# Weights loaded ahead of their stage, and a retention scan split between DVE and Pool, in an eight-core transformer kernel

## The chip, the cores and the metric

The kernel runs on the 8 cores of one Trainium2 chip, one launch, without communication between cores: cores 0 to 3 work on one latent sequence each, cores 4 to 7 on eight context sequences each. All run the same program on 2048 tokens. The metric is device microseconds of the slowest core. A run has a state: in the slow one, the cores of a die (0 to 3, or 4 to 7) show a lower granted TensorE clock and take some per cent longer. Names of engines: PE multiplies matrices, DVE (vector) and ACT (scalar) work element by element, Pool (GpSimd) can do so too but only issues DMAs in the kernel before, and SP issues the other DMAs. A DMA is a copy between the chip's main memory and SBUF, the memory on the core.

## The reference, cut to what matters

```python
def trunk_layer(x, cond, lp, cache=None, pos=None):      # 4 layers
    h = rms_norm(x, lp['g_pre_mix']) * (1 + sc1) + sh1
    gq, gk, gv, rq, rk, rv, rg, wq, wk, wv = project(h, lp['w_in'])
    glob = ...   # global attention
    win  = ...   # windowed attention
    ret, s_f, s_b = bidir_retention(rq32, rk32, rv32, lg_f, lg_b, ...)
    ret = head_rms(ret) * silu(rg)
    mixed = concat([glob, ret, win]) @ lp['w_out']
    x = x + gt1 * rms_norm(mixed, lp['g_post_mix'])
    ...          # SwiGLU feed-forward, gated residual

def retention_direction(q, k, v, log_gamma, s0):          # 16 chunks of 128 tokens
    def step(s, qkv):
        o = (q k^T * inner_decay) v + (q s) * q_decay     # needs the state before the chunk
        s = s * chunk_decay + (k * k_decay)^T v           # and passes it on
        return s, o
    return lax.scan(step, s0, chunks)
```

The forward direction walks the chunks 0 to 15, the backward one 15 to 0.

## The kernel before

Per layer the stages are: statistics; keys and values (PE needs `hg`, the normalised input, and a weight slot); queries and attention; retention pass A (decayed keys, values, one `U` per chunk); the scan over the chunks; retention pass B; output projection; feed-forward. Barriers, in which each engine waits for all others and for all DMAs, stand after the statistics, the attention, the retention, the output projection and the feed-forward; there is none inside the retention, between pass A, the scan and pass B.

Weights come through `wload`, in pieces, into one of three slots. Every piece writes the same `Buf`, so each waits until the piece before it has landed:

```python
    def wload(pieces, slot=None):
        ...
        for dv, src in pieces:
            S.dma('pool', dv(wslot[i]), src, writes=[WS[i]], semname=f"w{i}")
```

The loads stand in program order at the head of the stage that uses them, after the barrier, in the queue of Pool, which does nothing else. The scan runs on DVE, one direction after the other; partitions 0 to 63 hold the forward state and 64 to 127 the backward one:

```python
for d, rows, order in ((0, slice(0, 64), list(range(16))), (1, slice(64, 128), list(range(15, -1, -1)))):
    for idx, c in enumerate(order):
        S.op('act', ... activation(out=STb[rows, c, :], in_=srun[rows, :], func=AF.Copy) ...)   # state for pass B
        S.op('dve', ... tensor_tensor(out=U[rows, c, :], in0=U[rows, c, :], in1=srun[rows, :], op=ALU.add) ...)
        S.op('dve', ... tensor_tensor(out=U[rows, c, :], in0=U[rows, c, :], in1=gam[rows, :], op=ALU.mult) ...)
        if idx < 15:
            S.op('dve', ... tensor_scalar(out=srun[rows, :], in0=U[rows, c, :], scalar1=tabs[...], op0=ALU.mult) ...)
# pass B, first uses: emit_h(...) on DVE and ACT, rq projection on PE, then
S.mm(ps[ob]..., qs..., STb[:, c, ...], False, True, reads=[QS, STB[c]], ...)      # c = 0 first
...
S.barrier()
for c in range(6):                       # output projection: 14 pieces of w_out, then PE may start
    S.dma('pool', wo[0:64, c, :], w_out_d[...], writes=[WO], semname='wo')
    S.dma('pool', wo[64:128, c, :], w_out_d[...], writes=[WO], semname='wo')
...
```

The softmax here doesn't subtract the row's maximum and nothing guards it: scores larger than these inputs give would overflow.

Of the kernel before, what the change touches and what calls it, by code (L numbers as in the profile page):

```python
# [8 lines left out]
ALU = mybir.AluOpType  # L9
# [109 lines left out]
def build(stop=None):  # L119
# [202 lines left out]
    def normrope(l, g, gcol, ropeT, ROPE, final_fn):  # L322
        for p in normrope_ph(l, g, gcol, ropeT, ROPE, final_fn):
            p()

    def ck(name):
        if stop == name:
            raise _Stop()

    try:  # L330
        ck('prologue')
        emit_mod(0)
        ck('mod0')
        for l in range(L):
# [4 lines left out]
            with nc.sbuf_tensor(f"kTg{l}", [128, 2, 2304], BF16) as kTg, nc.sbuf_tensor(f"kTw{l}", [128, 2, 2304], BF16) as kTw, \  # L339
# [11 lines left out]
                for kvh in range(2):  # L351
# [4 lines left out]
                ck('s1a')  # L356
                wt, WT = wload([
                    (lambda s_: wview(s_, 512)[:, :, 0:64], wsrc(w_in_d, l, GK, 64)),
                    (lambda s_: wview(s_, 512)[:, :, 64:128], wsrc(w_in_d, l, WK, 64)),
                    (lambda s_: wview(s_, 512)[:, :, 128:192], wsrc(w_in_d, l, GK + 64, 64)),  # L360
                    (lambda s_: wview(s_, 512)[:, :, 192:256], wsrc(w_in_d, l, WK + 64, 64)),
                    (lambda s_: wview(s_, 512)[:, :, 256:384], wsrc(w_in_d, l, GV, 128)),
                    (lambda s_: wview(s_, 512)[:, :, 384:512], wsrc(w_in_d, l, WV, 128)),
                ], slot=0)
                for g in range(NG):
# [15 lines left out]
                    for kvh in range(2):  # L381
# [3 lines left out]
                        def fin(kn, KN, kvh=kvh, gs=gs):  # L385
# [6 lines left out]
                ck(f's1_{l}')  # L392
                w0, W0 = wload([(lambda s_, h=h: wview(s_, 512)[:, :, h * 128:h * 128 + 64], wsrc(w_in_d, l, GQ + h * 64, 64)) for h in range(4)] +
                               [(lambda s_, h=h: wview(s_, 512)[:, :, h * 128 + 64:h * 128 + 128], wsrc(w_in_d, l, WQ + h * 64, 64)) for h in range(4)], slot=1)
                w1, W1 = wload([(lambda s_, h=h: wview(s_, 512)[:, :, (h - 4) * 128:(h - 4) * 128 + 64], wsrc(w_in_d, l, GQ + h * 64, 64)) for h in (4, 5)] +
                               [(lambda s_, h=h: wview(s_, 512)[:, :, (h - 4) * 128 + 64:(h - 4) * 128 + 128], wsrc(w_in_d, l, WQ + h * 64, 64)) for h in (4, 5)], slot=2)

                def qproj_prep(g):
# [20 lines left out]
                def attn(g, nxt):  # L419
# [3 lines left out]
                    def npt():  # L423
                        i = pc[0] % 4; pc[0] += 1
                        return i
                    deferred = []

# [121 lines left out]
            with nc.sbuf_tensor(f"rkT{l}", [128, 2, NT], BF16) as rkT, nc.sbuf_tensor(f"rv{l}", [128, 16, 256], BF16) as rv, \  # L549
# [11 lines left out]
                kdec = rtab[:, 1024:1536]  # L561
                gam = rtab[:, 1536:1792]
                lg = rsm[:, 0:8]; lgmix = rsm[:, 8:12]; kd8 = rsm[:, 16:24]; g8 = rsm[:, 24:28]
                S.op('act', lambda e: e.activation(out=lg, in_=sm(l, 82, 8), func=AF.Exp, scale=-1.0), reads=[SMALLS], writes=[RSM])
# [16 lines left out]
                for d in range(2):  # L581
# [4 lines left out]
                     reads=[RSM], writes=[RTAB])  # L586
                w0, W0 = wload([(lambda s, h=h, d=d: wview(s, 512)[:, :, h * 128 + d * 64:h * 128 + d * 64 + 64], wsrc(w_in_d, l, RK + h * 64, 64))
                                for h in range(4) for d in range(2)], slot=0)
                w1, W1 = wload([(lambda s: wview(s, 512)[:, :, 0:256], wsrc(w_in_d, l, RV, 256)),
                                (lambda s: wview(s, 512)[:, :, 256:512], wsrc(w_in_d, l, RK, 256))], slot=1)  # L590
                wv0 = wview(w0, 512); wv1 = wview(w1, 512)
                for g in range(NG):
# [32 lines left out]
                    for b in range(4):  # L625
                        if b + 1 < 4:
                            a1_(b + 1)
                        a2_(b)
                ck(f'ra{l}')
                S.dma('sp', srun[0:64, :], st0_d[l, 0], writes=[SRUN[0]], semname='st0a')  # L630
                S.dma('sp', srun[64:128, :], st0_d[l, 1], writes=[SRUN[1]], semname='st0b')
                for d, rows, order in ((0, slice(0, 64), list(range(16))), (1, slice(64, 128), list(range(15, -1, -1)))):
                    for idx, c in enumerate(order):
                        S.op('act', lambda e: e.activation(out=STb[rows, c, :], in_=srun[rows, :], func=AF.Copy), reads=[SRUN[d]], writes=[STB[c]])
                        S.op('dve', lambda e: e.tensor_tensor(out=U[rows, c, :], in0=U[rows, c, :], in1=srun[rows, :], op=ALU.add), reads=[UU[c], SRUN[d]], writes=[UU[c]])
                        S.op('dve', lambda e: e.tensor_tensor(out=U[rows, c, :], in0=U[rows, c, :], in1=gam[rows, :], op=ALU.mult), reads=[UU[c], RTAB], writes=[UU[c]])
                        if idx < 15:
                            cn = order[idx + 1]
                            kc_ = (T_KF if d == 0 else T_KB) + cn
                            S.op('dve', lambda e: e.tensor_scalar(out=srun[rows, :], in0=U[rows, c, :], scalar1=tabs[rows, kc_:kc_ + 1], scalar2=None, op0=ALU.mult),  # L640
                                 reads=[UU[c], TABS], writes=[SRUN[d]])
                for c in range(16):
                    S.dma('sp', ost_d[l, c], U[:, c, :], reads=[UU[c]], semname='ost')
                ck(f'rec{l}')
                w0, W0 = wload([(lambda s, h=h, d=d: wview(s, 512)[:, :, h * 128 + d * 64:h * 128 + d * 64 + 64], wsrc(w_in_d, l, RQ + h * 64, 64))
                                for h in range(4) for d in range(2)], slot=2)
                w1, W1 = wload([(lambda s: wview(s, 512)[:, :, 0:256], wsrc(w_in_d, l, RG, 256))], slot=0)
                wv0 = wview(w0, 512); wv1 = wview(w1, 512)
                for g in range(NG):
# [29 lines left out]
                    def b2_(b, g=g):  # L679
# [4 lines left out]
                        for h in range(4):  # L684
                            S.mm(ps[ob][:, h * 64:(h + 1) * 64], ad[:, h * 128:(h + 1) * 128], rv[:, c, h * 64:(h + 1) * 64], True, False,
                                 reads=[AD, RV_], writes=[PS[ob]])
                            S.mm(ps[ob][:, h * 64:(h + 1) * 64], qs[:, h * 128:(h + 1) * 128], STb[:, c, h * 64:(h + 1) * 64], False, True,
                                 reads=[QS, STB[c]], writes=[PS[ob]])
                        sq_, SQ_ = ntf()
# [28 lines left out]
                    for t_ in range(4 + 2):  # L718
# [4 lines left out]
                        if 0 <= t_ - 2 < 4:  # L723
                            b3_(t_ - 2)
                    S.dma('sp', mscr_d[g, :, 6:8, :], rmt[:], reads=[RMT], semname='ms')
                S.barrier()
            ck(f'r{l}')
            with nc.sbuf_tensor(f"wo{l}", [128, 8, 1024], BF16) as wo, nc.sbuf_tensor(f"mgl{l}", [128, 2, 8, GT], BF16) as mgl, \
                    nc.sbuf_tensor(f"mx{l}", [128, 8, GT], F32) as mx:
                WO = Buf("wo"); MGL = [Buf("mgl0"), Buf("mgl1")]; MX = [Buf(f"mx{j}") for j in range(8)]  # L730
                for c in range(6):
                    S.dma('pool', wo[0:64, c, :], w_out_d[l, c * 64:(c + 1) * 64, :], writes=[WO], semname='wo')
                    S.dma('pool', wo[64:128, c, :], w_out_d[l, 640 + c * 64:640 + (c + 1) * 64, :], writes=[WO], semname='wo')
                S.dma('pool', wo[:, 6, :], w_out_d[l, 384:512, :], writes=[WO], semname='wo')
                S.dma('pool', wo[:, 7, :], w_out_d[l, 512:640, :], writes=[WO], semname='wo')
                for g in range(NG):
# [3 lines left out]
                    for dc in range(8):  # L740
                        pn = "A" if dc % 2 == 0 else "S0"
                        for c in range(8):
                            S.mm(ps[pn][:], wo[:, c, dc * 128:(dc + 1) * 128], mgl[:, mi, c, :], c == 0, c == 7, reads=[WO, MGL[mi]], writes=[PS[pn]])
                        S.op('act', lambda e: e.activation(out=mx[:, dc, :], in_=ps[pn][:], func=AF.Copy), reads=[PS[pn]], writes=[MX[dc]])
# [9 lines left out]
            with nc.sbuf_tensor(f"h2{l}", [128, 8, 1024], BF16) as h2, nc.sbuf_tensor(f"hid{l}", [128, 11, 1024], BF16) as hid, \  # L754
                    nc.sbuf_tensor(f"ff{l}", [128, 8, 1024], F32) as ff:
                H2 = Buf("h2"); HID = [Buf(f"hid{i}") for i in range(11)]; FF = [[Buf(f"ff{j}_{t}") for t in range(2)] for j in range(8)]
                for half in range(2):
# [42 lines left out]
                    for t in range(2):  # L800
# [4 lines left out]
                        for j in range(8):  # L805
                            tt, TT = ntf()
                            S.op('dve', lambda e: e.scalar_tensor_tensor(out=tt[:], in0=ff[:, j, ts], scalar=coef[l][:, 24 + j:25 + j], op0=ALU.mult, in1=rstdA[:, gs], op1=ALU.mult),  # L807
                                 reads=[FF[j][t], COEF[l], RA[g]], writes=[TT])
                            S.op('dve', lambda e: e.tensor_tensor(out=xT[:, j, gs], in0=xT[:, j, gs], in1=tt[:], op=ALU.add), reads=[X[g][j], TT], writes=[X[g][j]])  # L809
                S.barrier()  # L810
    except _Stop:
# [156 lines left out]
```

## Time and profile before

| | before |
|---|---|
| time, 6 runs | 8509.22 us median (8499.23 to 8523.8) |
| busy: PE, ACT, DVE, Pool | 63%, 44%, 26%, 5% |
| granted TensorE clock, all cores | 0.81 to 0.82 |

The shares of busy time are averages over stages with different limits, so they don't say what the change can win. The waits do. These lines are from the waits of the kernel before, slowest core (engine, what it was to write, line, what it waited for: us in all, times, longest):

```profile
PE psR L77 <- ACT hg L274: 394.5, 28, 57.2
PE psA L77 <- DMA wo<-w_out: 230.8, 4, 58.5
PE psR L77 <- DMA wslot<-w_in: 203.8, 4, 52.0
PE psA L77 <- DMA wslot<-w_in: 195.8, 4, 51.0
```

Three waits for weights occur once in each of the 4 layers. The first line is a sum over several places; its longest single wait, 57.2 us, is the scan.

How much of such a wait can be won is read from the timeline: what else would have been ready, and when? At the output projection (start, duration, engine, line, what, and in brackets the idle time before it and its releaser):

```profile
1468.85 0.79 SPq L95 DMA_DIRECT2D mgl<-mscr  x2
1469.37 0.54 POOL L95 DMA_DIRECT2D wo<-w_out  x1 [216.41 <-DMA mscr<-rmt]
1477.11 0.53 POOL L95 DMA_DIRECT2D wo<-w_out  x1 [7.20 <-DMA wo<-w_out]
1480.49 0.52 POOL L95 DMA_DIRECT2D wo<-w_out  x1 [2.85 <-DMA wo<-w_out]
...
1519.61 0.53 POOL L95 DMA_DIRECT2D wo<-w_out  x1 [3.85 <-DMA wo<-w_out]
1523.66 3.57 PE L77 MATMUL psA<-mgl,wo 128*128 128x512 bf16 x8 [58.45 <-DMA wo<-w_out]
```

One issue per 3.2 to 4.4 us after the first gap, each waiting for the landing of the one before. The other input, `mgl` (the concatenated head outputs), was issued first and takes 5.1 us (page, DMA issues). At the key/value projection (first two lines) and at pass A the other input is `hg`, and it was ready long before the weights:

```profile
158.65 6.43 ACT L274 ACTIVATE hg<-tf,mod 128x512 bf16<-128x512 f32 x8 [11.21 <-DVE tf L271]
196.81 3.57 PE L77 MATMUL psA<-hg,wslot 128*128 128x512 bf16 x8 [50.98 <-DMA wslot<-w_in]
...
1130.59 6.43 ACT L274 ACTIVATE hg<-tf,mod 128x512 bf16<-128x512 f32 x8 [1.22 <-DVE tf L271]
1162.47 5.85 PE L77 MATMUL psR<-hg,wslot 128*128 128x512 bf16 x16 [51.74 <-DMA wslot<-w_in]
```

The scan of the same layer, first step, then the end, and pass B's first use of the state:

```profile
1252.03 0.41 DVE L635 TENSOR_TENSOR U<-U,srun 64x256 f32<-64x256 f32 x1
1252.55 0.42 DVE L636 TENSOR_TENSOR U<-U,rtab 64x256 f32<-64x256 f32 x1
1253.44 0.34 DVE L640 TENSOR_SCALAR srun<-U,tabs_sb 64x256 f32<-64x256 f32 x1 [0.47 <-ACT STb L634]
...
1301.95 5.39 DVE L271 SCALAR_TENSOR_TENSOR tf<-xT_sb,coef,rstdA 128x512 f32<-128x512 f32 x8
1309.38 9.43 PE L77 MATMUL psR<-hg,wslot 128*128 128x512 bf16 x32 [56.84 <-ACT hg L274]
1322.78 0.19 PE L77 MATMUL psO<-STb,tb 128*128 128x64 bf16 x1
```

DVE executes in order, so the `h` of pass B (L271) stands behind all 32 steps of the scan: 49.9 us, 1.56 us a step.

### The profile page before, as it was taken

What the parts mean: (1) busy time and instruction counts of PE and PEld (TensorE: products, weight loads), DVE (VectorE), ACT (ScalarE), POOL (GpSimd) and SP (SyncE); (2) the same over time, 40 slices, a digit from 0 to 9 for tenths busy, and PEclk for the clock granted to TensorE, in tenths of its full rate; (3) what the DMA queues carried; (4) which work ended last, traced back from release to release, by engine and by line L of the source; (5) the groups of instructions that cost most, each with busy time, mean ns of one, the idle gap of its engine ahead of it and who ended that gap; (6) DMA issues with size and microseconds to landing.
All of it is one profiled execution on the core that took longest, in us unless ns stands there. A gap on an engine that the chain in (4) does not pass through costs nothing.

```text
span 8509.3 us, 86765 instructions; the slowest of 8 cores (8482.7 to 8509.3 us)
## 1 busy us (share of the span) xinstructions
PE 5320.0 (63%) x26992; PEld 2366.6 (28%) x26992; DVE 2250.3 (26%) x4163; ACT 3729.1 (44%) x6586; POOL 448.8 (5%) x533
## 2 busy tenths in 40 slices
PE   1477743598557773368936776337893676544887
PEld 0133321143223331123412332212341233221333
DVE  0312124212332213322132221432213222152232
ACT  1566633312356663342235666333214666533321
POOL 1000000011100000001100000000110000000000
PEclk8688876799778886679967988668995788876898
DMA  7111120164301112125521111213552000111445
GB/s 125 32 19 19 24 22 28 30 77 61 47 22 21 23 19 32 25 36 71 64 42 20 19 19 26 26 29 40 65 65 44 1 5 8 17 18 33 56 57 91
DMA packets 544142, 314.24 MB, mean 37 GB/s; under 512 B 185296, under 2 KB 519888, under 8 KB 540624
## 3 DMA queue, kind: packets, MB, share of 16 engines
q0 software_dynamic: 502160, 223.64, 22.1%
q1 hardware_dynamic: 41536, 85.05, 2.9%
q8 instruction: 231, 3.78, 0.2%
q14 instruction: 215, 1.76, 0.1%
HBM read 481.92 MB, written 50.33 MB: 63 GB/s over the span
## 4 chain that ended last, share of the span: by engine, by line
PE 52%; ACT 19%; DVE 10%; issue 10%; DMA 8%; ACTq 1%; DVEq 0%; POOL 0%; POOLq 0%; SPq 0%
PE psS L77 17%; PE psA L77 13%; PE psO L77 11%; PE psR L77 7%; ACT pT L461 4%; PE psM L77 3%; DMA wslot<-w_in 3%; ACT hg L274 3%; DMA wo<-w_out 2%; ACT pT L456 2%; DMA wslot<-w_mod 1%; ACT tb L260 1%; DVE tf L807 1%; ACT pT L504 1%; DVE xT_sb L809 1%
## 5 line engine op out<-in xcount | busy, mean ns | idle before, releaser
L77 PE MATMUL psO<-pT,vall 128*128 128x512 bf16 (+1 forms) x2832 | 847.1, 347 | 743.6 <-ACT pT L461 359.7
L461 ACT ACTIVATE pT<-psS,tabs_sb 128x512 bf16<-128x512 f32 x1344 | 901.2, 687 | 383.5 <-PE psS L77 370.3
L77 PE MATMUL psR<-pT,cbf_sb 128*128 128x512 bf16 (+1 forms) x2832 | 856.5, 350 | 0.0
L77 PE MATMUL psA<-h,wslot 128*128 128x512 bf16 x2816 | 677.1, 384 | 205.5 <-ACT h L765 130.3
L77 PE MATMUL psS<-qTg,kTg 128*128 128x512 bf16 x1728 | 690.2, 410 | 12.2 <-ACT qTg L410 12.2
L77 PEld LDWEIGHTS psO<-pT,vall 128*128 128x128 bf16 x2832 | 257.5, 104 | 1520.9 <-issue 1508.9
L77 PE MATMUL psM<-tb,cbf_sb 128*128 128x512 bf16 x768 | 351.4, 478 | 526.1 <-ACT tb L260 301.9
L77 PE MATMUL psS<-h,wslot 128*128 128x512 bf16 x2816 | 665.4, 379 | 0.0
L783 ACT ACTIVATE tf<-psA 128x512 f32<-128x512 f32 x352 | 210.4, 598 | 964.5 <-PE psA L77 939.3
L77 PE MATMUL psR<-hg,wslot 128*128 128x512 bf16 x768 | 238.4, 479 | 598.8 <-ACT hg L274 394.5
L784 DVE TENSOR_TENSOR hid<-tf,psS 128x512 bf16<-128x512 f32 x352 | 241.9, 687 | 1337.6 <-PE psS L77 1251.7
L77 PE MATMUL psA<-hg,wslot 128*128 128x512 bf16 x896 | 284.0, 474 | 366.4 <-DMA wslot<-w_in 195.8
L77 PEld LDWEIGHTS psA<-h,wslot 128*128 128x128 bf16 x2816 | 277.0, 99 | 549.2 <-issue 226.3
L274 ACT ACTIVATE hg<-tf,mod 128x512 bf16<-128x512 f32 x512 | 369.9, 723 | 116.0 <-DVE tf L271 74.3
L456 ACT ACTIVATE pT<-psS,tabs_sb 128x256 bf16<-128x256 f32 x768 | 354.4, 474 | 115.1 <-PE psS L77 71.5
L77 PEld LDWEIGHTS psS<-h,wslot 128*128 128x128 bf16 x2816 | 275.9, 98 | 333.8 <-issue 2.8
L271 DVE SCALAR_TENSOR_TENSOR tf<-xT_sb,coef,rstdA 128x512 f32<-128x512 f32 x512 | 344.3, 743 | 10.5 <-DMA okT<-tf 10.1
L77 PE MATMUL psO<-hid,wslot 128*128 128x512 bf16 x1408 | 324.8, 379 | 0.0
L77 PE MATMUL psS<-hid,wslot 128*128 128x512 bf16 x1408 | 324.8, 379 | 0.0
L507 DVE TENSOR_TENSOR pT<-pT,cbf_sb 128x128 bf16<-128x128 bf16 x360 | 79.0, 220 | 812.2 <-ACT pT L504 811.0
L77 PEld LDWEIGHTS psM<-tb,cbf_sb 128*128 128x128 bf16 x768 | 76.9, 100 | 776.3 <-issue 754.9
L77 PEld LDWEIGHTS psR<-hg,wslot 128*128 128x128 bf16 x768 | 86.9, 118 | 740.4 <-issue 698.8
(146 smaller groups left out, 6983.5 us busy)
## 6 DMA issues: line engine op xcount, KB each, us to landing
wslot<-w_gate_up POOLq DMA_DIRECT2D x160, 512.0 KB, 6.2
wslot<-w_mod POOLq DMA_DIRECT2D x48, 1024.0 KB, 8.3
wslot<-w_down POOLq DMA_DIRECT2D x64, 704.0 KB, 7.1
wslot<-w_in POOLq DMA_DIRECT2D x128, 128.0 KB, 3.5
mgl<-mscr SPq DMA_DIRECT2D x16, 1024.0 KB, 5.1
mscr<-mg SPq DMA_DIRECT2D x16, 768.0 KB, 3.3
xT_sb<-xT SPq DMA_DIRECT2D x32, 256.0 KB, 19.6
ropeT<-rope SPq DMA_DIRECT2D x8, 1024.0 KB, 4.9
```

Source lines behind the costliest of these rows:

```text
L77: inst = self.eng[e].matmul(out, lhsT=lhsT, rhs=rhs, start=start, stop=stop)
L260: S.op('act', lambda e: e.activation(out=q[:], in_=src_fn(j), func=AF.Square), reads=[SRC[j]], writes=[Q])
L271: S.op('dve', lambda e: e.scalar_tensor_tensor(out=t[:], in0=xT[:, j, gs], scalar=coef[l][:, a_off + j:a_off + j + 1], op0=ALU.mult, in1=r ...
L274: S.op('act', lambda e: e.activation(out=hg[hi][:, j, :], in_=t[:], func=AF.Identity, bias=modt[l][:, b_off + j:b_off + j + 1]), reads=[T, ...
L456: S.op('act', lambda e: e.activation(out=pT[:, pi, qh * 256:(qh + 1) * 256], in_=ps[sn][:, qh * 256:(qh + 1) * 256], func=AF.Exp, bias=tco ...
L461: S.op('act', lambda e: e.activation(out=pT[:, pi, :], in_=ps[sn][:], func=AF.Exp, bias=tcol(bc)), reads=[PS[sn], TABS], writes=[PT[pi]])
L504: S.op('act', lambda e: e.activation(out=pT[:, pi, 0:n], in_=ps[sn][:, 0:n], func=AF.Exp), reads=[PS[sn]], writes=[PT[pi]])
L507: S.op('dve', lambda e: e.tensor_tensor(out=pT[:, pi, j * 128:(j + 1) * 128], in0=pT[:, pi, j * 128:(j + 1) * 128], in1=mprev[i % 2], op=A ...
L783: S.op('act', lambda e: e.activation(out=sa[:], in_=ps["A"][:], func=AF.Silu), reads=[PS["A"]], writes=[SA])
L784: S.op('dve', lambda e: e.tensor_tensor(out=hid[:, fi, ts], in0=sa[:], in1=ps["S0"][:], op=ALU.mult), reads=[SA, PS["S0"]], writes=[HID[fi]])
L807: S.op('dve', lambda e: e.scalar_tensor_tensor(out=tt[:], in0=ff[:, j, ts], scalar=coef[l][:, 24 + j:25 + j], op0=ALU.mult, in1=rstdA[:, g ...
L809: S.op('dve', lambda e: e.tensor_tensor(out=xT[:, j, gs], in0=xT[:, j, gs], in1=tt[:], op=ALU.add), reads=[X[g][j], TT], writes=[X[g][j]])
```

## The change

Its intent: load each stage's weights while the stage before still computes, and halve the scan by running its two directions at once, the forward one on DVE and the backward one on Pool. The diff, cut to its core:

```diff
+    def load_s1w(l):                      # key/value weights, slot 0
+    def load_passA(l):                    # pass A's weights, slots 1 and 2
+    def load_wo_half(l, half, slot):      # half of w_out: 4 of the 8 row blocks, in a weight slot
         emit_mod(0)
+        load_s1w(0)
 ...     # last attention group:
+                    if nxt is None:
+                        load_passA(l)
 ...     # head of the retention stage:
+                PW['pb0'] = wload([... RQ ...], slot=0)        # pass B's query weights
-                w0, W0 = wload([... RK ...], slot=0)
-                w1, W1 = wload([... RV, RK ...], slot=1)
+                w0, W0 = PW['pa0']; w1, W1 = PW['pa1']
 ...     # after pass A, before the scan:
+                PW['pb1'] = wload([... RG ...], slot=1)
+                load_wo_half(l, 0, 2)
-                for d, rows, order in ((0, slice(0, 64), ...), (1, slice(64, 128), ...)):
-                    for idx, c in enumerate(order):
+                chains = ((0, slice(0, 64), list(range(16)), 'dve'), (1, slice(64, 128), list(range(15, -1, -1)), 'pool'))
+                for idx in range(16):
+                    for d, rows, order, eng in chains:
+                        c = order[idx]
+                        if eng == 'dve':
+                            S.op('act', ... STb[rows, c, :] <- srun[rows, :] ...)
+                        else:
+                            S.op('pool', ... tensor_copy(out=STb[rows, c, :], in_=srun[rows, :]) ...)
+                        S.op(eng, ... add ...); S.op(eng, ... mult by gam ...)
+                        if idx < 15: S.op(eng, ... tensor_scalar to srun ...)
 ...     # end of pass B:
+                load_wo_half(l, 1, 0)
                 S.barrier()
-                for c in range(6):
-                    S.dma('pool', wo[0:64, c, :], ...)           # 14 pieces
 ...     # end of the feed-forward:
+                if l + 1 < L:
+                    load_s1w(l + 1)
                 S.barrier()
```

The query weights move to the head of the key/value stage in program order; Pool's queue reaches them at the same place as before.

More of the change, by code (lines that the diff above doesn't have):

```diff
@@ L324, in normrope, with wo_view @@
             p()
+    PW = {}
+    def load_s1w(l):
+        PW['s1'] = wload([
+            (lambda s_: wview(s_, 512)[:, :, 0:64], wsrc(w_in_d, l, GK, 64)),
+            (lambda s_: wview(s_, 512)[:, :, 64:128], wsrc(w_in_d, l, WK, 64)),
+            (lambda s_: wview(s_, 512)[:, :, 128:192], wsrc(w_in_d, l, GK + 64, 64)),
+            (lambda s_: wview(s_, 512)[:, :, 192:256], wsrc(w_in_d, l, WK + 64, 64)),
+            (lambda s_: wview(s_, 512)[:, :, 256:384], wsrc(w_in_d, l, GV, 128)),
+            (lambda s_: wview(s_, 512)[:, :, 384:512], wsrc(w_in_d, l, WV, 128)),
+        ], slot=0)
+    def load_passA(l):
+        PW['pa0'] = wload([(lambda s_, h=h, d=d: wview(s_, 512)[:, :, h * 128 + d * 64:h * 128 + d * 64 + 64], wsrc(w_in_d, l, RK + h * 64, 64))
+                           for h in range(4) for d in range(2)], slot=1)
+        PW['pa1'] = wload([(lambda s_: wview(s_, 512)[:, :, 0:256], wsrc(w_in_d, l, RV, 256)),
+                           (lambda s_: wview(s_, 512)[:, :, 256:512], wsrc(w_in_d, l, RK, 256))], slot=2)
+    def wo_view(slot):
+        return slot[:, 0:4096].rearrange("p (c e) -> p c e", c=4)
+    def load_wo_half(l, half, slot):
+        pieces = []
+        for c in range(half * 4, half * 4 + 4):
+            cc = c % 4
+            if c < 6:
+                pieces.append((lambda s_, cc=cc: wo_view(s_)[0:64, cc, :], w_out_d[l, c * 64:(c + 1) * 64, :]))
+                pieces.append((lambda s_, cc=cc: wo_view(s_)[64:128, cc, :], w_out_d[l, 640 + c * 64:640 + (c + 1) * 64, :]))
+            elif c == 6:
+                pieces.append((lambda s_, cc=cc: wo_view(s_)[:, cc, :], w_out_d[l, 384:512, :]))
+            else:
+                pieces.append((lambda s_, cc=cc: wo_view(s_)[:, cc, :], w_out_d[l, 512:640, :]))
+        PW['wo%d' % half] = wload(pieces, slot=slot)
     def ck(name):
@@ L356, in build @@
                 ck('s1a')
-                wt, WT = wload([
-                    (lambda s_: wview(s_, 512)[:, :, 0:64], wsrc(w_in_d, l, GK, 64)),
-                    (lambda s_: wview(s_, 512)[:, :, 64:128], wsrc(w_in_d, l, WK, 64)),
-                    (lambda s_: wview(s_, 512)[:, :, 128:192], wsrc(w_in_d, l, GK + 64, 64)),
-                    (lambda s_: wview(s_, 512)[:, :, 192:256], wsrc(w_in_d, l, WK + 64, 64)),
-                    (lambda s_: wview(s_, 512)[:, :, 256:384], wsrc(w_in_d, l, GV, 128)),
-                    (lambda s_: wview(s_, 512)[:, :, 384:512], wsrc(w_in_d, l, WV, 128)),
-                ], slot=0)
+                w0, W0 = wload([(lambda s_, h=h: wview(s_, 512)[:, :, h * 128:h * 128 + 64], wsrc(w_in_d, l, GQ + h * 64, 64)) for h in range(4)] +
+                               [(lambda s_, h=h: wview(s_, 512)[:, :, h * 128 + 64:h * 128 + 128], wsrc(w_in_d, l, WQ + h * 64, 64)) for h in range(4)], slot=1)
+                w1, W1 = wload([(lambda s_, h=h: wview(s_, 512)[:, :, (h - 4) * 128:(h - 4) * 128 + 64], wsrc(w_in_d, l, GQ + h * 64, 64)) for h in (4, 5)] +
+                               [(lambda s_, h=h: wview(s_, 512)[:, :, (h - 4) * 128 + 64:(h - 4) * 128 + 128], wsrc(w_in_d, l, WQ + h * 64, 64)) for h in (4, 5)], slot=2)
+                wt, WT = PW['s1']
                 for g in range(NG):
@@ L392, in build @@
                 ck(f's1_{l}')
-                w0, W0 = wload([(lambda s_, h=h: wview(s_, 512)[:, :, h * 128:h * 128 + 64], wsrc(w_in_d, l, GQ + h * 64, 64)) for h in range(4)] +
-                               [(lambda s_, h=h: wview(s_, 512)[:, :, h * 128 + 64:h * 128 + 128], wsrc(w_in_d, l, WQ + h * 64, 64)) for h in range(4)], slot=1)
-                w1, W1 = wload([(lambda s_, h=h: wview(s_, 512)[:, :, (h - 4) * 128:(h - 4) * 128 + 64], wsrc(w_in_d, l, GQ + h * 64, 64)) for h in (4, 5)] +
-                               [(lambda s_, h=h: wview(s_, 512)[:, :, (h - 4) * 128 + 64:(h - 4) * 128 + 128], wsrc(w_in_d, l, WQ + h * 64, 64)) for h in (4, 5)], slot=2)
                 def qproj_prep(g):
@@ L562, in build @@
                 gam = rtab[:, 1536:1792]
+                PW['pb0'] = wload([(lambda s_, h=h, d=d: wview(s_, 512)[:, :, h * 128 + d * 64:h * 128 + d * 64 + 64], wsrc(w_in_d, l, RQ + h * 64, 64))
+                                   for h in range(4) for d in range(2)], slot=0)
                 lg = rsm[:, 0:8]; lgmix = rsm[:, 8:12]; kd8 = rsm[:, 16:24]; g8 = rsm[:, 24:28]
@@ L586, in build @@
                      reads=[RSM], writes=[RTAB])
-                w0, W0 = wload([(lambda s, h=h, d=d: wview(s, 512)[:, :, h * 128 + d * 64:h * 128 + d * 64 + 64], wsrc(w_in_d, l, RK + h * 64, 64))
-                                for h in range(4) for d in range(2)], slot=0)
-                w1, W1 = wload([(lambda s: wview(s, 512)[:, :, 0:256], wsrc(w_in_d, l, RV, 256)),
-                                (lambda s: wview(s, 512)[:, :, 256:512], wsrc(w_in_d, l, RK, 256))], slot=1)
+                w0, W0 = PW['pa0']; w1, W1 = PW['pa1']
                 wv0 = wview(w0, 512); wv1 = wview(w1, 512)
@@ L628, in build @@
                         a2_(b)
+                PW['pb1'] = wload([(lambda s_: wview(s_, 512)[:, :, 0:256], wsrc(w_in_d, l, RG, 256))], slot=1)
+                load_wo_half(l, 0, 2)
                 ck(f'ra{l}')
@@ L631, in build @@
                 S.dma('sp', srun[64:128, :], st0_d[l, 1], writes=[SRUN[1]], semname='st0b')
-                for d, rows, order in ((0, slice(0, 64), list(range(16))), (1, slice(64, 128), list(range(15, -1, -1)))):
-                    for idx, c in enumerate(order):
-                        S.op('act', lambda e: e.activation(out=STb[rows, c, :], in_=srun[rows, :], func=AF.Copy), reads=[SRUN[d]], writes=[STB[c]])
-                        S.op('dve', lambda e: e.tensor_tensor(out=U[rows, c, :], in0=U[rows, c, :], in1=srun[rows, :], op=ALU.add), reads=[UU[c], SRUN[d]], writes=[UU[c]])
-                        S.op('dve', lambda e: e.tensor_tensor(out=U[rows, c, :], in0=U[rows, c, :], in1=gam[rows, :], op=ALU.mult), reads=[UU[c], RTAB], writes=[UU[c]])
+                UH = [[Buf(f"uf{c}") for c in range(16)], [Buf(f"ub{c}") for c in range(16)]]
+                for c in range(16):
+                    UH[0][c].w = UU[c].w; UH[1][c].w = UU[c].w
+                STH = [[Buf(f"sf{c}") for c in range(16)], [Buf(f"sb{c}") for c in range(16)]]
+                chains = ((0, slice(0, 64), list(range(16)), 'dve'), (1, slice(64, 128), list(range(15, -1, -1)), 'pool'))
[3 more added lines that the diff above has]
+                        if eng == 'dve':
+                            S.op('act', lambda e: e.activation(out=STb[rows, c, :], in_=srun[rows, :], func=AF.Copy), reads=[SRUN[d]], writes=[STH[d][c]])
+                        else:
+                            S.op('pool', lambda e: e.tensor_copy(out=STb[rows, c, :], in_=srun[rows, :]), reads=[SRUN[d]], writes=[STH[d][c]])
+                        S.op(eng, lambda e: e.tensor_tensor(out=U[rows, c, :], in0=U[rows, c, :], in1=srun[rows, :], op=ALU.add), reads=[UH[d][c], SRUN[d]], writes=[UH[d][c]])
+                        S.op(eng, lambda e: e.tensor_tensor(out=U[rows, c, :], in0=U[rows, c, :], in1=gam[rows, :], op=ALU.mult), reads=[UH[d][c], RTAB], writes=[UH[d][c]])
                         if idx < 15:
@@ L639, in build @@
                             kc_ = (T_KF if d == 0 else T_KB) + cn
-                            S.op('dve', lambda e: e.tensor_scalar(out=srun[rows, :], in0=U[rows, c, :], scalar1=tabs[rows, kc_:kc_ + 1], scalar2=None, op0=ALU.mult),
-                                 reads=[UU[c], TABS], writes=[SRUN[d]])
+                            S.op(eng, lambda e: e.tensor_scalar(out=srun[rows, :], in0=U[rows, c, :], scalar1=tabs[rows, kc_:kc_ + 1], scalar2=None, op0=ALU.mult),
+                                 reads=[UH[d][c], TABS], writes=[SRUN[d]])
                 for c in range(16):
-                    S.dma('sp', ost_d[l, c], U[:, c, :], reads=[UU[c]], semname='ost')
+                    S.dma('sp', ost_d[l, c], U[:, c, :], reads=[UH[0][c], UH[1][c]], semname='ost')
                 ck(f'rec{l}')
-                w0, W0 = wload([(lambda s, h=h, d=d: wview(s, 512)[:, :, h * 128 + d * 64:h * 128 + d * 64 + 64], wsrc(w_in_d, l, RQ + h * 64, 64))
-                                for h in range(4) for d in range(2)], slot=2)
-                w1, W1 = wload([(lambda s: wview(s, 512)[:, :, 0:256], wsrc(w_in_d, l, RG, 256))], slot=0)
+                w0, W0 = PW['pb0']; w1, W1 = PW['pb1']
                 wv0 = wview(w0, 512); wv1 = wview(w1, 512)
@@ L687, in b2_ @@
                             S.mm(ps[ob][:, h * 64:(h + 1) * 64], qs[:, h * 128:(h + 1) * 128], STb[:, c, h * 64:(h + 1) * 64], False, True,
-                                 reads=[QS, STB[c]], writes=[PS[ob]])
+                                 reads=[QS, STH[0][c], STH[1][c]], writes=[PS[ob]])
                         sq_, SQ_ = ntf()
@@ L725, in build @@
                     S.dma('sp', mscr_d[g, :, 6:8, :], rmt[:], reads=[RMT], semname='ms')
+                load_wo_half(l, 1, 0)
                 S.barrier()
             ck(f'r{l}')
-            with nc.sbuf_tensor(f"wo{l}", [128, 8, 1024], BF16) as wo, nc.sbuf_tensor(f"mgl{l}", [128, 2, 8, GT], BF16) as mgl, \
+            with nc.sbuf_tensor(f"mgl{l}", [128, 2, 8, GT], BF16) as mgl, \
                     nc.sbuf_tensor(f"mx{l}", [128, 8, GT], F32) as mx:
-                WO = Buf("wo"); MGL = [Buf("mgl0"), Buf("mgl1")]; MX = [Buf(f"mx{j}") for j in range(8)]
-                for c in range(6):
-                    S.dma('pool', wo[0:64, c, :], w_out_d[l, c * 64:(c + 1) * 64, :], writes=[WO], semname='wo')
-                    S.dma('pool', wo[64:128, c, :], w_out_d[l, 640 + c * 64:640 + (c + 1) * 64, :], writes=[WO], semname='wo')
-                S.dma('pool', wo[:, 6, :], w_out_d[l, 384:512, :], writes=[WO], semname='wo')
-                S.dma('pool', wo[:, 7, :], w_out_d[l, 512:640, :], writes=[WO], semname='wo')
+                MGL = [Buf("mgl0"), Buf("mgl1")]; MX = [Buf(f"mx{j}") for j in range(8)]
+                wo_t = [wo_view(PW['wo0'][0]), wo_view(PW['wo1'][0])]; WO_B = [PW['wo0'][1], PW['wo1'][1]]
                 for g in range(NG):
@@ L742, in build @@
                         for c in range(8):
-                            S.mm(ps[pn][:], wo[:, c, dc * 128:(dc + 1) * 128], mgl[:, mi, c, :], c == 0, c == 7, reads=[WO, MGL[mi]], writes=[PS[pn]])
+                            S.mm(ps[pn][:], wo_t[c // 4][:, c % 4, dc * 128:(dc + 1) * 128], mgl[:, mi, c, :], c == 0, c == 7, reads=[WO_B[c // 4], MGL[mi]], writes=[PS[pn]])
                         S.op('act', lambda e: e.activation(out=mx[:, dc, :], in_=ps[pn][:], func=AF.Copy), reads=[PS[pn]], writes=[MX[dc]])
```

## The prediction

> **What bounds it now.** 8509 us on the slowest core, clock 0.81. Attention and feed-forward, most of the span, are untouched; the change aims at idle PE between stages. In the waits of the slowest core, PE stood still for DMA of weights in three places per layer (4 layers): 195.8 us before the key/value projection (`psA<-hg,wslot`), 203.8 us before retention pass A (`psR<-hg,wslot`), 230.8 us before the output projection (`wo<-w_out`). Each piece waits for the piece before it: in the timeline Pool issues a w_in piece per 4.2 us and a w_out piece per 3.87 us. A fourth hole is the retention scan: 32 steps of 1.58 us on DVE (1252.0 to 1301.9 us), then hg; PE idles 57 us.
>
> **Gains, from the timeline, not the whole idle time** (hg must be ready anyway):
> - Key/value projection: hg is ready at 165.2, PE starts at 196.8 (layer 0): 31 us; layers 1 to 3: 2262.4 against 2291.7, 29 us. Sum 117. The next layer's load (6 pieces, about 26 us) just fits in the 30 us tail after the last feed-forward matmul.
> - Pass A: hg ready at 1137.1, PE starts at 1162.5: 25 x 4 = 101.
> - Output projection: barrier at 1468.8, PE starts at 1523.7; what is left is the mgl load, 5.1 us plus issue: 48 x 4 = 192. The second half of the weights loads in the last 25 us of pass B, again a narrow fit.
> - Query and pass B weights gain nothing: they already load during earlier stages.
>
> **The split scan: about nothing.** DVE is free after 16 x 1.58 = 25 us instead of 50. But the Pool chain stands in Pool's queue *behind* the 8 serialized pieces of half of w_out (and one of RG), which can start only when pass A frees their slots: 8 x 3.87 puts the chain's start about 30 us after pass A. Pool then needs 15 full steps before chunk 0, which pass B wants first. No Pool arithmetic is in this trace. The Trainium skill, "GPSIMD Engine Reference", section 3.1, states about 2.6 cycles per element at 1.2 GHz for tensor_tensor; for 256 elements I estimate 0.6 us each, and with copy, scalar op and semaphore waits 2.7 us a step (range 2 to 4). Chunk 0 is ready near 30 + 15 x 2.7 = 71 us; before, pass B's first use came at 70 us (50 scan, 7 hg, 12 projection and scores). Break-even, -10 to +20 us per layer.
>
> **Sum.** 8510 - 117 - 101 - 192 = 8100; plus about 25 us for scan loss, late halves and contention at the start: **8125 us**, range 8060 to 8215. Chances: faster by over 2% 0.96, within 2% 0.03, slower 0.01.
>
> **What would show it.** The three DMA waits of PE vanish; pass A starts 21 us after the attention barrier, the output projection 7 us after its barrier. Pool's arithmetic starts about 30 us after pass A's last matmul, behind the w_out issues; PE gets a new wait on Pool (`psO<-STb`), 20 to 40 us per layer, in place of most of the 57 us on hg. Attention and feed-forward windows keep their lengths.
>
> **What would make it wrong.** Pool steps over 4 us (a large fixed cost per instruction): each extra us costs 60 us in all. Steps under 2 us: up to 60 us more gain. Barriers that now wait for prefetched weights, if pieces take over 5 us there. Pass A's prefetch delaying the w_mod loads in attention (I expect two heads of slack).

## The result, and the profile after

| | runs | median (range) |
|---|---|---|
| before | 20 | 8506.74 us (8499.23 to 8530.15) |
| changed | 10 | 8128.40 us (8123.24 to 8134.47) |

The ratio is 0.9552, with a 95% interval of 0.9544 to 0.9560. (A ratio is the mean time of one kernel's fast runs over that of the other's of the same rounds, so not quite the ratio of the medians.) The prediction was 8125 us.

The waits of the changed kernel, core 5 (the core that was the slowest in the profile of before). The three waits of PE for weights are gone; in place of the one for `wo` stands a short one for `mgl`; and there is a new one, on Pool:

```profile
PE psR L77 <- ACT hg L274: 402.2, 32, 31.9
PE psO L77 <- POOL STb L674: 128.7, 4, 32.3
PE psA L77 <- DMA mgl<-mscr: 37.9, 4, 10.5
```

The timeline of the same core, first layer, where the key/value projection, pass A and the output projection start:

```profile
158.69 6.42 ACT L274 ACTIVATE hg<-tf,mod 128x512 bf16<-128x512 f32 x8 [11.21 <-DVE tf L271]
165.26 3.57 PE L77 MATMUL psA<-hg,wslot 128*128 128x512 bf16 x8 [19.38 <-ACT hg L274]
...
1096.78 6.42 ACT L274 ACTIVATE hg<-tf,mod 128x512 bf16<-128x512 f32 x8 [1.22 <-DVE tf L271]
1103.34 6.52 PE L77 MATMUL psR<-hg,wslot 128*128 128x512 bf16 x16 [26.48 <-ACT hg L274]
...
1418.13 0.79 SPq L95 DMA_DIRECT2D mgl<-mscr  x2
1425.26 3.57 PE L77 MATMUL psA<-mgl,wslot 128*128 128x512 bf16 x8 [10.48 <-DMA mgl<-mscr]
```

And the scan. Pass A's last matmul starts at 1194.40; DVE is done with its half at 1218.77, where its next instruction, L271, starts (25 us after pass A instead of 50); but Pool's queue first works through the pieces of w_out:

```profile
1194.30 0.87 POOL L95 DMA_DIRECT2D wslot<-w_in  x1 [80.32 <-PE psO L77]
1195.16 0.54 POOL L95 DMA_DIRECT2D wslot<-w_out  x1
1202.47 0.53 POOL L95 DMA_DIRECT2D wslot<-w_out  x1 [6.76 <-DMA wslot<-w_out]
...
1222.70 0.52 POOL L95 DMA_DIRECT2D wslot<-w_out  x1 [2.92 <-DMA wslot<-w_out]
1223.26 1.14 POOL L674 CAST STb<-srun 64x256 bf16<-64x256 f32 x1
...
1227.27 0.40 POOL L674 CAST STb<-srun 64x256 bf16<-64x256 f32 x1
1227.63 0.72 POOL L675 TENSOR_TENSOR U<-U,srun 64x256 f32<-64x256 f32 x1
1228.50 0.72 POOL L676 TENSOR_TENSOR U<-U,rtab 64x256 f32<-64x256 f32 x1
1229.39 0.92 POOL L680 TENSOR_SCALAR srun<-U,tabs_sb 64x256 f32<-64x256 f32 x1 [0.17 <-POOL U L676]
...
1271.99 0.39 POOL L674 CAST STb<-srun 64x256 bf16<-64x256 f32 x1
1272.53 0.21 PE L77 MATMUL psO<-STb,tb 128*128 128x64 bf16 x1 [32.02 <-POOL STb L674]
```

The Pool chain starts 29 us after pass A's last matmul (27 to 29 us over the 4 layers), a step takes 3.18 us from one CAST to the next (1227.27 to 1230.45), and the state of chunk 0 comes last of all. PE, which had everything else for pass B, waits 32 us for it.

The table splits one core's span by the starts of such marks in the timeline (core 5 in both kernels, us, sum of the 4 layers; the differences are worked out from it).

| stretch | before | after | difference |
|---|---|---|---|
| barrier to first key/value matmul | 188.7 | 68.7 | -120.0 |
| keys, queries, attention | 3665.0 | 3653.5 | -11.5 |
| attention's barrier to first matmul of pass A | 180.8 | 84.5 | -96.3 |
| pass A | 359.3 | 362.8 | +3.5 |
| pass A's last `U` to pass B's first matmul | 226.6 | 126.0 | -100.6 |
| from there to the first use of the state | 53.8 | 186.0 | +132.2 |
| rest of pass B | 585.9 | 584.2 | -1.7 |
| retention's barrier to first output projection | 217.1 | 22.3 | -194.8 |
| output projection | 649.9 | 648.3 | -1.6 |
| feed-forward | 2014.1 | 2016.3 | +2.2 |
| its tail, statistics, output | 217.5 | 217.2 | -0.3 |

The three prefetches give 411 us (120.0 + 96.3 + 194.8). The scan, as one stretch from pass A to the first use of the state, takes 280.4 us before and 312.0 after: it *lost* 31.6 us, 7.9 us a layer. The 11.5 us in the attention stretch is less than the difference of two cores of the kernel before in it (3665.0 on core 5, 3649.9 on core 0), so nothing is read into it.

### The profile page after: what moved, and what is told of

It reads as the page before. It is cut to its first block, busy times and chain, and to the rows that moved or that the text cites. A ratio compares the mean times of both kernels' runs of the same rounds, so it can differ in the third digit from the quotient of the medians.

```text
span 8140.6 us, 86727 instructions; the slowest of 8 cores (8111.2 to 8140.6 us)
## 1 busy us (share of the span) xinstructions
PE 5343.4 (66%) x26992; PEld 2373.5 (29%) x26992; DVE 2177.6 (27%) x3975; ACT 3700.7 (45%) x6522; POOL 628.7 (8%) x785
## 4 chain that ended last, share of the span: by engine, by line
PE 54%; ACT 20%; issue 10%; DVE 10%; DMA 3%; POOL 2%; ACTq 1%; DVEq 0%; POOLq 0%; SPq 0%
PE psS L77 18%; PE psA L77 13%; PE psO L77 11%; PE psR L77 7%; ACT pT L491 4%; PE psM L77 4%; ACT hg L274 3%; ACT pT L486 2%; DMA wslot<-w_mod 1%; ACT tb L260 1%; DVE tf L271 1%; DVE tf L842 1%; ACT pT L534 1%; DVE xT_sb L844 1%; ACT pTc L520 1%
## 5 line engine op out<-in xcount | busy, mean ns | idle before, releaser
L271 DVE SCALAR_TENSOR_TENSOR tf<-xT_sb,coef,rstdA 128x512 f32<-128x512 f32 x512 | 344.5, 743 | 10.3 <-DMA okT<-tf 9.9
L95 POOL DMA_DIRECT2D wslot<-w_gate_up x192 | 167.9, 875 | 1822.1 <-DMA wslot<-w_gate_up 590.2
```

The source lines that it names most:

```text
L95: inst = self.eng[e].dma_start(out=out, in_=in_)
L271: S.op('dve', lambda e: e.scalar_tensor_tensor(out=t[:], in0=xT[:, j, gs], scalar=coef[l][:, a_off + j:a_off + j + 1], op0=ALU.mult, in1=r ...
```

## The experiments

The total came out 3 us from the prediction, but a total can be right by cancelling errors, and the odd part is that an optimisation in the change costs time. The theory to test: (Q) the split loses because the Pool chain stands in Pool's queue behind w_out's pieces, not because Pool is slow as such. Rivals: (S) Pool's own slowness is the whole cost; (L) Pool and DVE block each other when their chains overlap, so a better place in the queue would gain less than it seems. And for the prefetches: do they add up, or does freed time reappear as another wait?

The chips of the experiments were slow for many runs, on one die or both. So times below are of single runs in which one die or both kept their clock, and the mechanism is read from the stage table of a core of such a die; there the first use repeats to some tenths of a microsecond, while a long stretch differs more between cores: the output projection, summed over the layers, by 8 us between cores 5 and 0 of the kernel before (649.9 and 642.0 us). The changed kernel was not run again in these sessions; the kernel before was, and in its undisturbed runs it took 8499.7 to 8502.3 us in the session of the next four runs, 4 to 7 us under its median above. So a difference from 8128.4 us is uncertain by some 5 us. "First use" is the mean distance from pass A's last `U` to pass B's first matmul with the state: 70.1 us before, 78.0 in the changed kernel.

### The scan ahead of w_out in Pool's queue

```diff
-                load_wo_half(l, 0, 2)        # before the scan
+                load_wo_half(l, 0, 2)        # after the scan
```

> The changed kernel, with the first half of w_out issued after the scan instead of before it; nothing else. Theory Q (place in Pool's queue): the Pool chain started 29 us after pass A only because the w_out pieces stood before it; it now starts about 1 us after pass A, and pass B's first use of the state comes at about 50 us after pass A instead of 78, so 28 us less per layer: about 8016 us. Theory L (lock): now the Pool chain overlaps the DVE chain (25 us), and instructions with two SBUF inputs on both engines block each other, so steps stretch on both (Pool over 3.18 us, DVE over 1.56 us); the first use comes at 60 to 65 us, and the time is about 8070 us. Rival S (Pool's own slowness is the whole cost, its place does not matter): no change, 8128.

Measured: on die 0, undisturbed in all four runs, the cores took 8024 to 8042 us (die 1 was at a lower clock, up to 8361 us). First use at 56.1 us. So 22 us a layer less than in the changed kernel: S, which expected no change, is out. But it is not the 28 us of Q either: 56.1 us lies between Q's 50 and L's 60 to 65. What ate the rest is in the timeline (core 0): where the chains overlap, DVE and Pool hold each other up.

```profile
1194.71 0.86 DVE L679 TENSOR_SCALAR srun<-U,tabs_sb 64x256 f32<-64x256 f32 x1 [0.48 <-ACT STb L671]
1195.62 0.72 POOL L675 TENSOR_TENSOR U<-U,rtab 64x256 f32<-64x256 f32 x1 [0.20 <-DVE srun L679]
1195.67 0.95 DVE L674 TENSOR_TENSOR U<-U,srun 64x256 f32<-64x256 f32 x1
...
1227.72 5.78 POOL L673 CAST STb<-srun 64x256 bf16<-64x256 f32 x1
1227.86 5.38 DVE L271 SCALAR_TENSOR_TENSOR tf<-xT_sb,coef,rstdA 128x512 f32<-128x512 f32 x8
1233.47 0.72 POOL L674 TENSOR_TENSOR U<-U,srun 64x256 f32<-64x256 f32 x1
...
1250.12 0.19 PE L77 MATMUL psO<-STb,tb 128*128 128x64 bf16 x1 [2.08 <-POOL STb L673]
```

Here DVE's tensor_scalar takes 0.86 us instead of 0.34 and its add 0.95 instead of 0.41. A DVE step is now 2.16 us (1193.30 to 1227.86 for 16) instead of 1.56. Then DVE issues the eight instructions of the next `h` back to back, and the one CAST that Pool had started 0.14 us earlier ends only after the eighth: 5.78 us instead of 0.39. The Trainium skill, "SBUF — State Buffer", section "Who interferes with whom", says that a DVE instruction with two SBUF inputs contends with a GpSimd instruction that reads SBUF; it calls the ports that the two engines share an exclusive lock, and says of DVE's 2-port modes that the engine that issues second fully blocks. This trace agrees that one engine blocks the other (which of them came first is taken up in the last section): L271 has two SBUF inputs, and the CAST beside its eight instructions lasts 5.4 us longer. In each of the 4 layers one step of the Pool chain, beside these eight, takes 8.0 to 8.7 us instead of 3.18 (from the starts of the CASTs); that is most of the 6 us above Q's 50. So L is the rest of the answer. PE now waits only 2.08 us for Pool: everything else that it needs, with DVE's half of the scan, is ready just 2 us earlier.

### The scan back on DVE, prefetches kept

```diff
-                for idx in range(16):
-                    for d, rows, order, eng in chains: ...
+                for d, rows, order in ((0, slice(0, 64), ...), (1, slice(64, 128), ...)):   # as before, all on DVE
```

> The changed kernel with the scan undone: all 32 steps on DVE, one direction after the other, as before; the three prefetches kept. My theory: the split as built costs 8 us per layer (first use of the state at 78 us after pass A against 70), so undoing it gives about 8097 us. Rival (the split is a gain of the 25 us per layer that it takes off DVE): about 8228 us.

Measured: 8093.89 us (both dies at 0.83), first use at 70.0 us as in the kernel before. The rival is out: as built, the split costs the change 34 us (8128.4 - 8093.9, two sessions), which agrees with the 31.6 us of the stage table. The prefetches alone are worth 408 us (8501.5, the median of the three undisturbed runs of the kernel before that were taken together with this one, less 8093.9), which agrees with the 411 of the stage table.

### The split alone

```diff
 # the kernel before, plus:
-                for d, rows, order in (...): ...                # scan on DVE
+                w0, W0 = wload(... RQ ...); w1, W1 = wload(... RG ...)   # moved ahead of the scan
+                chains = (... 'dve'), (... 'pool'); ...         # split scan
```

> The kernel before, with only the split scan; pass B's own weight loads are issued ahead of the scan so that they don't queue behind the Pool chain, and no w_out pieces stand before it. Theory Q without a lock: first use of the state at 50 us after pass A instead of 70, 20 us less per layer: about 8425 us. Theory L: first use at 60 to 65 us, about 8475 us. Rival S: Pool's chain is as late as in the changed kernel, 78 us, about 8540 us.

Measured: 8452.31 us in the one run with both dies at their clock, 49 us less than before in the same session (8501.5); first use at 56.2 us. The same split that costs 34 us in the changed kernel wins 49 us where no w_out pieces stand in Pool's queue. Again between Q and L, with the same 56 us.

### The changed kernel without the early w_out loads

```diff
-                load_wo_half(l, 0, 2)
-                load_wo_half(l, 1, 0)
+                (own tensor wo, 14 pieces after the barrier, as before)
```

> The changed kernel without the early w_out loads (own tensor, loaded after the retention barrier as before). If the 195 us that the output projection's wait shrank by were the whole effect of this prefetch, the time rises to about 8322 us. My theory: this prefetch also delays the Pool chain, so without it the scan gets 15 to 28 us shorter per layer and the time rises to only 8210 to 8262 us.

Measured: 8237.76 us (both dies at 0.82 to 0.83), 109 us more than the changed kernel. In the stage table (core 0) the wait at the output projection grows by 199.2 us (221.5 against 22.3) and the scan shrinks by 88.2 us (223.8 against 312.0). So the early w_out loads win 195 us and lose nearly half of it at once, by their place in the queue.

### The other two prefetches, each undone

```diff
-        load_s1w(0) ...  load_s1w(l + 1)          # first run: key/value weights after the barrier again
-                        load_passA(l)             # second run: pass A's weights after the barrier again,
-                PW['pb0'] = wload(...)            #   pass B's query weights behind them
```

> The changed kernel with the key/value weights loaded where they were before (after the barrier, behind the cached keys in Pool's queue). My theory (the gains of the prefetches add up, stage by stage): the stretch from the barrier to PE's first key/value matmul goes back from 17 to about 47 us in each layer and nothing else moves: about 8128 + 120 = 8248 us. Rival (the time that the prefetch freed reappears as another wait in the same layer, so each prefetch alone is worth less): clearly under 8230 us.

> The changed kernel with pass A's weights loaded where they were before (after the attention barrier), and pass B's query weights behind them. My theory: the stretch from the attention barrier to PE's first matmul of pass A goes back from 21 to about 45 us in each layer: about 8128 + 96 = 8224 us. Rival as for the key/value run: clearly under 8205 us.

Measured, key/value run: 8226.9 to 8234.6 us on die 0 in the run whose die 0 was undisturbed (die 1 of the same run was at a lower clock, 8276.79 us), 8222.7 to 8234.9 us on die 1 in another. The stretch itself grew by 117.3 us (186.0 against 68.7, core 0), as expected. Set against 8128.4 us this is about 106 us, less than expected and just at the rival's line; but 8128.4 us is the slowest of eight cores, and here only four are undisturbed. Compared alike, the mean of the four cores (8231.2 and 8229.0 us) is 112 to 114 us above the mean of all cores of the changed kernel in its ten runs (8117.0 us). That is the 117 us of the stretch within 3 to 5 us, so these runs give the rival no support. In the stage table the output projection seems shorter (639.6 us, against 648.3 on core 5 of the changed kernel), but core 4 of the changed kernel has 639.2 us too.

Measured, pass A run: 8214.76 us, 86 us more than the changed kernel, and the stretch itself grew by 91.7 us (176.2 against 84.5, core 4); the mean of the eight cores is 90 us above the 8117.0 us. No other stretch grew: in these two runs, no freed time came back as a new wait that the table shows.

### All on DVE, with two instructions a step

A step needs no instruction of its own for `srun`: the scale by `tabs` and the add fit in one scalar_tensor_tensor, and ACT can scale while it copies the state. A first version had Pool use the new step too; it did not compile. This one has both directions interleaved on DVE, ahead of w_out's issue:

```diff
+   S.op('act', activation(out=STb[rows, c, :], in_=U[rows, cp, :], func=AF.Copy, scale=tabs[rows, kc_:kc_ + 1]))
+   S.op('dve', scalar_tensor_tensor(out=U[rows, c, :], in0=U[rows, cp, :], scalar=tabs[...], op0=mult, in1=U[rows, c, :], op1=add))
+   S.op('dve', tensor_tensor(out=U[rows, c, :], in0=U[rows, c, :], in1=gam[rows, :], op=mult))
```

> The changed kernel with w_out issued after the scan and the scan all on DVE, both directions interleaved, with two instructions a step instead of three (scale and add in one; the scaled copy for the state goes to ACT). No arithmetic on Pool, so no lock. My theory: 32 steps of about 1.1 us, DVE free at 35 us, pass B's first use of the state at about 56 us after pass A, as in the run with the Pool chain first: about 8040 us. If the lock were not what stretched that run, but the chain of waits itself, this one would not reach 1.1 us a step.

Measured: 8017 to 8031 us on die 0 (8116.11 us on die 1, at a lower clock), first use at 53.3 us. The step, in the timeline of core 0:

```profile
1205.29 0.48 DVE L678 SCALAR_TENSOR_TENSOR U<-U,tabs_sb 64x256 f32<-64x256 f32 x1
1205.88 0.42 DVE L680 TENSOR_TENSOR U<-U,rtab 64x256 f32<-64x256 f32 x1
1206.33 0.48 DVE L678 SCALAR_TENSOR_TENSOR U<-U,tabs_sb 64x256 f32<-64x256 f32 x1
```

1.04 us a step, and the tensor_tensor takes 0.42 us as in the kernel before. One engine with two instructions a step is slightly ahead of two engines with three and four at their best place (first use 53.3 against 56.1 us). The totals point the same way (die 0 8017 to 8031 against 8024 to 8042 us), but the kernel before, run beside each of the two, also took 7 us less here (8494.3 against 8501.5 us, medians of its undisturbed runs), so they don't show it alone.

### The forward half inside pass A

The forward direction can follow pass A chunk by chunk, as soon as a `U` is there. DVE was busy for 27 of pass A's 90 us in the kernel before (windows of the profile).

```diff
                         a2_(b)
+                        if 4 * g + b >= 1: scan(0, 4 * g + b - 1)      # forward step, one chunk behind
 ...
+                for idx in range(16): scan(1, idx)                     # backward steps alone after pass A
```

> As the run before, but the forward direction's steps are issued inside pass A, one chunk behind its U, and only the 16 backward steps stand after pass A, all on DVE. Expected: 16 steps of about 1.15 us, pass B's first use at 38 to 41 us after pass A (78 in the changed kernel), pass A longer by less than 3 us per layer: 7970 to 7990 us, faster than both kernels. If pass A's DVE or ACT were the limit there, pass A grows by 10 us or more per layer and the gain is gone.

Measured: 7992 to 8018 us on the undisturbed die of four runs, above the 7970 to 7990 expected. First use at 41.4 us, about as expected, but pass A took 99.1 to 100.1 us in the first three layers (core 0; the profile fell in a slow run), about 9 us more than the changed kernel's 90.7 instead of under 3. In the timeline one forward step stood on DVE and ACT just ahead of each next group's `h`, and PE idled 8.9 us there instead of 7.0: some 6 us at the three places of a layer. How much of the rest is the lower clock of that run is not known. That suggested the last run, which moves only these steps:

```diff
-                        if 4 * g + b >= 1: scan(0, 4 * g + b - 1)
+                        for i in {0: (4 * g - 2, 4 * g - 1), 1: (4 * g,), 2: (4 * g + 1,), 3: ()}[b]: scan(0, i)   # if i >= 0
+                    # the last two forward steps go between the first backward ones
```

> As the run with the forward steps in pass A, but no forward step stands on DVE between the last block of a group and the next group's h (two steps go after the first block of the next group; the last two steps go between the first backward ones). In that run pass A had grown by 9 us per layer, and the trace shows the step's two DVE instructions (about 1.1 us) and ACT's copy ahead of the next h at each of the group boundaries, with PE idle 8.9 us there instead of 7.0. Expected: pass A within 3 us of 91 us, first use of the state at about 42 us after pass A, so 33 to 37 us less per layer than the changed kernel: about 7990 us on cores of an undisturbed die, 0.94 of before. If pass A stays at 99 us, the boundary was not the reason.

Measured: pass A 94.1 us a layer, first use at 41.2 us; 7996.72 us in the one run with both dies at their clock (0.83 to 0.84), and 7963 to 8002 us on the undisturbed die in the seven slow ones. The kernel before took 8496.33 and 8498.5 us in its undisturbed runs of the same session; 7996.72 over their mean is 0.941. That is one run, so no interval. Against the changed kernel's 8128.4 us it is 132 us less, from the scan alone. The outputs were correct. So pass A came 3 us above the changed kernel's, just outside the expected. As the other profile was a slow one, the undisturbed dies are the fair test: the mean of their cores went from between 8005 and 8011 us to between 7981 and 7994 us, some 20 us, which is the 5 us a layer by which pass A got shorter. So the place ahead of `h` was most of pass A's growth. Of the 3 us that stayed, PE's idle time at the three places makes some 2.5 (7.8 us each instead of 7.0); why it is still longer was not looked into.

## Why the prediction was right

| step of the prediction | predicted | measured |
|---|---|---|
| key/value prefetch | -117 | -120.0 |
| pass A prefetch | -101 | -96.3 |
| w_out prefetch, at its stage | -192 | -194.8 |
| query and pass B weights | nothing | attention stretch unchanged within scatter |
| start of the Pool chain after pass A | about 30 us | 27 to 29 us |
| a Pool step | 2.7 us (2 to 4) | 3.18 us |
| first use of the state after pass A | 71 us | 78.0 us |
| scan, per layer | -10 to +20 us | +7.9 us |
| PE's new wait on Pool | 20 to 40 us a layer | 32 us |
| time | 8125 (8060 to 8215) | 8128.4 |

It was right because the gains were not taken from the waits (630 us in all: 195.8 + 203.8 + 230.8) but from the timeline: the time between the moment when the *other* input was ready and the moment when PE started. That gave 410 us, and 411 came. The narrow fits held as well: the second half of w_out landed before the barrier (22.3 us for 4 layers from the barrier to PE).

It was also right that the split would win nothing, and for the stated reason, the order in Pool's queue; the run with that order changed shows it. The term that was off in size is the Pool step: 2.7 us was an estimate from the Trainium skill's 2.6 cycles per element ("GPSIMD Engine Reference", section 3.1); it is 3.18 us. The estimate for one tensor_tensor was 0.6 us, and the trace shows 0.72. Over the 15 steps before chunk 0 that is 7.2 us, about the difference of 71 and 78; two smaller terms cancel, an earlier start and a longer first step (below). In the sum it hid in the 25 us that were added for losses. That the total came so close, 3 us, is partly luck: the scan alone lost 31.6 us where 25 stood for all losses, and the sum started from 8510 us where the kernel before took 8506.7. The step is measured from start to start; the skill's "Perfetto Trace Analysis", section "GPSIMD Engine Instruction", says that a single span of this engine in a profile is not to be relied on.

The prediction does not mention the lock between DVE and Pool. From its own times (DVE free at 25 us, Pool's chain from 30 us on) the two hardly overlap, and so it went in this kernel, because the queue held Pool back. Only the first CAST meets the last of `h`'s instructions on DVE: it takes 1.1 to 2.7 us instead of 0.39, and the first step 4.0 to 5.5 us instead of 3.18 in the four layers (core 5). Whoever mends the queue meets the whole lock.

## What to carry to other kernels

Cost a prefetch by what else the consumer was waiting for, not by the length of its wait. An engine's queue is in order for everything in it: when compute moves to an engine that issues DMAs, look at what stands ahead of it there, and issue what is needed first (22 us a layer here). Before splitting a serial chain over two engines, ask whether it can have fewer instructions, or hide behind a stage that leaves the engine idle; here that gave about twice as much, 97 us (8093.9 us with the old scan on DVE less the last run's 7996.7, two sessions) against 49 us for the split alone at its best place (8501.5 - 8452.3; single undisturbed runs of each version), and no lock.

## What the Trainium skill lacked or had wrong

- "GPSIMD Engine Reference", section 4.1, calls one-input operations on this engine roughly line-rate. Here tensor_scalar on 64x256 f32, with one tensor input, took 0.92 us on Pool, more than the two-input tensor_tensor (0.72 us), and 2.7 times DVE's 0.345 us. The CAST with one input took 0.39 us. Measured from start to start the order is the same: 1.06, 0.87 to 0.89 and 0.36 us.
- "GPSIMD Engine Reference", section 3.1, gives 1.96 times DVE's time for a tensor_tensor of 2048 elements. At 256 elements it was 0.72 against 0.42 us, 1.7 times; but a dependent step of four Pool instructions took 3.18 us against 1.56 us for DVE's three. The page has no cost for short dependent chains on this engine.
- "SBUF — State Buffer", section "Who interferes with whom", describes the lock for pairs of instructions. No page says what a burst does: eight DVE instructions back to back kept one Pool CAST for 5.78 us instead of 0.39, though the CAST had started first by 0.14 us in the profile.
